# Routing tables, tile order and memory layout ahead of a mixture-of-experts loop

## The chip, the cores and the metric

The kernel runs on 1 core of one Trainium2 chip. The metric is the device time of one execution, from start to end, in microseconds (us); lower is better. Engines are PE (matmul), DVE (vector), ACT (scalar), POOL (GpSimd) and SP (which here only issues DMAs). POOL issues DMAs too.

## The reference

One decoder layer over 1024 prompt tokens and 8 sample tokens: S5 state space branch and sparse attention in parallel, an output projection with a post-norm, then a mixture of 32 experts, 4 of which each token uses. What the change touches is the expert routing:

```
logits = (x @ w_router).astype(F32) + b_router.astype(F32)
top_v, top_e = lax.top_k(logits, TOP_K)          # 4 experts of 32 for each token
...
counts = jnp.bincount(e, length=N_EXPERTS)
pcounts = (counts + blk - 1) // blk * blk
...
row_tok = jnp.full((rows,), n, jnp.int32).at[dest].set(tok_s)   # which token stands in which row
blk_e = jnp.minimum(jnp.searchsorted(pend, jnp.arange(n_blk) * blk, side='right'), N_EXPERTS - 1)
...
gate = jnp.minimum(gu[:, :D_FF], SWIGLU_LIMIT)   # per block: two products with the expert's weights
hh = (up + 1.0) * gate * jax.nn.sigmoid(SWIGLU_ALPHA * gate)
return hh @ w_down[ei] + b_down[ei]
```

## The kernel before

Tokens stand in 9 tiles: tiles 0 to 7 hold 128 prompt tokens each, tile NT = 8 holds the 8 sample tokens. The stages that matter run in this order.

**Output stage** (`post`). Three steps per tile: `glu(t)` (three tiles ahead), `outer(t)` (two halves of 24 products each, then DVE and ACT work for two norms, with the results `x1` and `hd` stored to DRAM) and `route(t)` (8 transposes of `h`, two ACT copies, the router products, then `choose`, nine small DVE steps to the top 4 experts, and a running count `cum`). The order on each engine is made by a planner. Tile 8 comes last. `mod` holds three rows of modulation; it is loaded for tile 0 and again, other values, for tile 8.

**Dispatch** (`dispatch`). From the counts: `rk`, the rank of each token within its expert (PE); the item table, one row of 4 numbers per work item, by some 30 small DVE steps; `slots`, called twice (a multiply-add to `sm`, a product `tmp` of 1152 numbers, its sum, a cast): once for the rows of the expert stage, once for `slot`, which only the last stage uses. Then 36 pairs of one-hot tiles `ol` and `ob` on DVE and 36 products into `ip` give `idx`, the token of each row. The item table goes to `tab` by way of DRAM (`tabd`), since it has to turn from 64 partitions into one.

**Expert loop** (`moe_raw`). Ahead of it, POOL issues, in this order: the load of `sel`, the loads of the first expert's gate and up weights into `raw[:,0:4]` (L110, eight of 1 MB), and zeros for `bc`, `st` and `ut`. Then a hand-synchronised section begins. SP goes into it first (L113): it waits for all that the section reads or writes, and then all engines start it. In it, POOL gathers tokens by `idx` (L421), ACT and DVE split weights into `hi` and `lo`, PE multiplies.

**Combine.** Gathers the rows back by `slot`, sums and norms; it already takes the sample's tile first.

**Memory.** Pools without a side are stacked from the left end of each partition, those with `side="right"` from the other. A left pool that closes gives its space to the next. So the pool of the output stage and the pool of the expert loop begin at the same byte. In bytes per partition, the output stage's pool begins with the two parts of `w_out` (65,536), `mod[0]`, `mod[1]`, `mod[2]` (4,096 each); the expert loop's begins with `sel` (2,048) and `raw` (98,304). The pool `di` of dispatch lies at the right end, and the last tiles of the expert loop's pool (`st`, `ut`, `sh`, `yt`, `bc`, `ic`) lie over it. A tile's first writer waits for the last readers of every tile that lay in any of its bytes (`reuse_waits="tile"`).

Of the kernel before, what the change touches and what calls it, by code (L numbers as in the profile page):

```python
# [22 lines left out]
D = 1024  # L23
# [59 lines left out]
def moe_raw(tc, x, wgu, wd, ydram, tab, idx, bsc, sel, ident, pools, NIT_MAX, NE=32):  # L83
# [10 lines left out]
    raw=sb.tile([128,6,4096],F,name="raw")  # L94
# [3 lines left out]
    st=sb.tile([128,2,2,256],F,name="st"); ut=sb.tile([128,2,2,256],F,name="ut")  # L98
    sh=sb.tile([128,2,512],F,name="sh")
    yt=sb.tile([128,2,1024],F,name="yt")  # L100
    bc=sb.tile([128,512],FR,name="bc")
    ic=sb.tile([128,2],I32,name="ic")
# [10 lines left out]
    with tc.tile_critical():  # L113
# [5 lines left out]
        def rawview(u):  # L119
            if u<16: return raw[:,u//4,u%4*1024:(u%4+1)*1024].rearrange("p (k f) -> p k f",k=2)  # L120
            C,k=DOWN[u-16]
            return raw[:,4+k//4].rearrange("p (k f) -> p k f",k=4)[:,k%4:k%4+2,C*512:(C+1)*512]
# [16 lines left out]
        with nc.Block() as block:  # L139
            @block.sync  # L140
            def _(eng):
                E=Eng(eng,nc,tab,W,NIT_MAX); i1=E.reg(1,1); i2=E.reg(2,1); pt=E.reg(W,W); ex=E.reg(); en=E.reg(); ep=E.reg(0); eq=E.reg(NE)
                def load(e,m):
                    if m<4:
                        src=wgu[bass.ds(e,1)].rearrange("o (k p) (h f) -> (o p) k h f",p=128,h=2)[:,:,:,m*256:(m+1)*256]
                        dst=raw[:,m].rearrange("p (k h f) -> p k h f",k=8,h=2)
                        for h in range(2): eng.dma_start(out=dst[:,:,h],in_=src[:,:,h]).then_inc(S['raw'][m],16)
                    else:
                        src=wd[bass.ds(e,1)].rearrange("o (k p) f -> (o p) k f",p=128)[:,(m-4)*4:(m-3)*4]
                        eng.dma_start(out=raw[:,m].rearrange("p (k f) -> p k f",k=4),in_=src).then_inc(S['raw'][m],32)  # L150
# [300 lines left out]
class K:  # L451
# [1360 lines left out]
    def post(self):  # L1812
# [4 lines left out]
        with ExitStack() as c:  # L1817
# [77 lines left out]
            def route(t):  # L1895
                n = rows(t)
                h = live.pop(t)
                ht = p.tile([128, 8, 128], F, name="ht")
                for k0 in (0, 4):
                    tp = q.tile([128, 4, 128], F, name="tph", bufs=1)  # L1900
                    for k in range(4):
                        pe.transpose(tp[:, k, :n], h[:n, (k0 + k) * 128:(k0 + k) * 128 + 128], self.ident[:n, :n])
                    A.activation(out=ht[:, k0:k0 + 4, :n], in_=tp[:, :, :n], func=AF.Copy)
                pr = q.tile([128, 32], F, name="pr", bufs=1)
                for k in range(8):
                    pe.matmul(pr[:n], lhsT=ht[:, k, :n], rhs=wr[:, k], start=k == 0, stop=k == 7)
                self.choose(t, n, pr, br)

            for t in range(AHEAD):
                glu(t)  # L1910
# [11 lines left out]
            for t in range(NT + 2):  # L1922
                if t == 1:
                    self.expert_bias(p)
                if t <= NT:
                    outer(t)
                if t + AHEAD <= NT:
                    glu(t + AHEAD)
                if t:
                    route(t - 1)  # L1930
# [6 lines left out]
    def dispatch_pools(self, ctx):  # L1937
# [15 lines left out]
        nc.sync.dma_start(out=self.tok, in_=self.i["k_token"])  # L1953
# [35 lines left out]
    def dispatch(self):  # L1989
# [4 lines left out]
        tabd = tc.dram_tile([65, 4], I32, name="tabd")  # L1994
        with ExitStack() as c:
            q = self.pool("diq", psum=True, ctx=c)

# [6 lines left out]
            for k, s in enumerate((7, 8, 6)):  # L2004
                v.tensor_scalar(out=ci[:, k], in0=rk[:, NTT], scalar1=float(2 ** s - 1), scalar2=None, op0=ALU.add)
                v.tensor_scalar(out=ci[:, k], in0=ci[:, k], scalar1=s, scalar2=None, op0=ALU.arith_shift_right)
            v.tensor_copy(out=cnt[:, 3], in_=rk[:, NTT])
            v.tensor_copy(out=cnt[:, 0:3], in_=ci)
            inc = p.tile([128, 4, 32], F, name="inc")
            exc = p.tile([128, 4, 32], F, name="exc")  # L2010
            for k in (0, 1, 3):
                v.tensor_tensor_scan(out=inc[:, k], data0=ones[:, 0:32], data1=cnt[:, k], initial=0.0, op0=ALU.mult, op1=ALU.add)
                v.tensor_tensor(out=exc[:, k], in0=inc[:, k], in1=cnt[:, k], op=ALU.subtract)

            n = 64
            m1 = p.tile([n, 32], F, name="m1")
            m2 = p.tile([n, 32], F, name="m2")
            v.tensor_scalar(out=m1, in0=exc[:n, 1], scalar1=row[:n], scalar2=None, op0=ALU.is_le)
            v.tensor_scalar(out=m2, in0=inc[:n, 1], scalar1=row[:n], scalar2=None, op0=ALU.is_gt)
            v.tensor_tensor(out=m1, in0=m1, in1=m2, op=ALU.mult)  # L2020
# [6 lines left out]
            v.tensor_tensor(out=j, in0=j, in1=pk[:, 4:5], op=ALU.mult)  # L2027
            it = p.tile([n, 4], F, name="it")

            v.tensor_scalar(out=it[:, 0:1], in0=pk[:, 4:5], scalar1=-31.0, scalar2=31.0, op0=ALU.mult, op1=ALU.add)  # L2030
            v.tensor_tensor(out=it[:, 0:1], in0=it[:, 0:1], in1=pk[:, 0:1], op=ALU.add)
            v.scalar_tensor_tensor(out=it[:, 1:2], in0=j, scalar=2.0, in1=pk[:, 2:3], op0=ALU.mult, op1=ALU.add)
            v.scalar_tensor_tensor(out=it[:, 2:3], in0=j, scalar=-4.0, in1=pk[:, 3:4], op0=ALU.mult, op1=ALU.add)
            v.tensor_scalar(out=it[:, 2:3], in0=it[:, 2:3], scalar1=2.0, scalar2=4.0, op0=ALU.max, op1=ALU.min)
            v.scalar_tensor_tensor(out=it[:, 3:4], in0=j, scalar=256.0, in1=pk[:, 5:6], op0=ALU.mult, op1=ALU.add)
            iti = p.tile([n, 4], I32, name="iti")
            v.tensor_copy(out=iti, in_=it)
            ni = p.tile([1, 4], I32, name="ni")
            v.tensor_copy(out=ni, in_=inc[0:1, 1, 31:32].to_broadcast([1, 4]))
# [7 lines left out]
            def slots(out, k, scale):  # L2047
                v.scalar_tensor_tensor(out=sm, in0=exc[:, k:k + 1].to_broadcast([128, NTT, 32]), scalar=scale, in1=rk[:, 0:NTT], op0=ALU.mult, op1=ALU.add)
# [5 lines left out]
            slots(vs, 0, 128.0)  # L2054
# [42 lines left out]
    def combine(self):  # L2097
# [3 lines left out]
        with ExitStack() as c:  # L2101
            p = self.pool("co", ctx=c)
            q = self.pool("coq", bufs=2, psum=True, ctx=c)
            row = lambda name, bufs: p.tile([128, D], F, name=name, bufs=bufs)

            def fetch(t):
                n = 128 if t < NT else B
                ys = []
                for k in range(4):
                    ys.append(row("y", 4 * LOOK + 8))  # L2110
                    g_.indirect_dma_start(out=ys[-1][:n], out_offset=None, in_=self.yd, in_offset=bass.IndirectOffsetOnAxis(ap=self.slot[:n, t, k:k + 1], axis=0))
# [35 lines left out]
            def weights(t, on):  # L2147
# [3 lines left out]
                pe.transpose(wt[:, :n], wr[:n, t], self.ident[:n, :n])  # L2151
# [20 lines left out]
            def rest(t, n, ys, x, pb, on):  # L2172

                acc, prev = row("acc", NTT), pb
                for k in range(on, 4):
                    v.scalar_tensor_tensor(out=acc[:n], in0=ys[k][:n], scalar=wk[:n, t, k:k + 1], in1=prev[:n], op0=ALU.mult, op1=ALU.add)  # L2176
# [143 lines left out]
```

## Time and profile before

| | |
|---|---|
| three runs | 3199.05, 3202.93, 3207.68 us (median 3202.93) |
| profiled execution | 3209.21 us, of which the span from first to last instruction is 3207.4 us |
| PE, DVE, ACT, POOL busy | 93%, 72%, 56%, 11% of the span |
| instructions | 51067 |

The profiled execution is 6.28 us above the median. The 1.8 us that are no part of its span lie around the first and the last instruction. All times in the text below are us from the start of the span.

### The profile page before, as it was taken

How to read it: one execution, taken by the hardware profiler on the slowest of the kernel's cores; microseconds unless marked ns; L12 is line 12 of the kernel's file. 1: busy time of each engine (PE TensorE's matmuls, PEld its weight loads, DVE VectorE, ACT ScalarE, POOL GpSimd, SP SyncE). 2: the span in 40 equal slices, each digit the busy share in tenths (PEclk: the TensorE clock that was granted, in tenths of full speed). 3: DMA queues.
4: the chain of work that ended last, by engine and by line, in shares of the span. 5: the costliest groups of instructions: out<-in, count | busy, mean ns of one | idle time of the engine just before them, and what ended most of it. 6: DMA issues, size and time to landing. Idle time of an engine off the chain costs nothing. (4 is left out here: it accounts for less than half of the span.)

```text
span 3207.4 us, 51067 instructions
## 1 busy us (share of the span) xinstructions
PE 2972.0 (93%) x15681; PEld 2380.6 (74%) x15682; DVE 2321.0 (72%) x4434; ACT 1785.9 (56%) x2824; POOL 358.7 (11%) x467
## 2 busy tenths in 40 slices
PE   7787899998999898599999999999999999999977
PEld 4555699976778586378887887888887888878752
DVE  5654846448777688688878868775689865796978
ACT  3332635456657643377667656564477654675751
POOL 1620121002311000100000000000000000000013
PEclk9888899988879799699999999999999999999988
DMA  8766343223512342798979869764289915792926
GB/s 287 250 219 226 126 124 106 85 74 83 132 29 65 126 152 80 264 335 288 315 228 369 277 230 360 233 238 139 77 281 371 337 68 190 242 368 100 350 84 275
DMA packets 445575, 656.33 MB, mean 205 GB/s; under 512 B 45455, under 2 KB 371072, under 8 KB 441265
## 3 DMA queue, kind: packets, MB, share of 16 engines
q1 hardware_dynamic: 418290, 535.40, 49.7%
q0 software_dynamic: 24464, 115.59, 10.4%
q10 hardware_dynamic: 2704, 3.85, 0.3%
q8 instruction: 64, 1.05, 0.1%
q14 instruction: 53, 0.43, 0.0%
HBM read 594.95 MB, written 68.73 MB: 207 GB/s over the span
## 5 line engine op out<-in xcount | busy, mean ns | idle before, releaser
L272 DVE TENSOR_TENSOR lo<-raw,hi 128x1024 fp32r<-128x1024 f32 x870 | 1030.9, 1221 | 307.3 <-ACT hi L199 302.3
L199 ACT ACTIVATE hi<-raw 128x1024 fp32r<-128x1024 f32 x870 | 916.3, 1060 | 491.9 <-PE pc L388 490.7
L386 PE MATMUL pc<-hi,X 128*128 128x512 f32 x1408 | 561.0, 398 | 4.7 <-DVE X L277 3.8
L388 PE MATMUL pc<-hi,X 128*128 128x512 f32 x1408 | 550.8, 391 | 0.0
L387 PE MATMUL pc<-lo,X 128*128 128x512 f32 x1408 | 549.8, 390 | 0.0
L386 PEld LDWEIGHTS pc<-hi,X 128*128 128x128 f32 x1408 | 265.2, 188 | 60.6 <-issue 8.9
L388 PEld LDWEIGHTS pc<-hi,X 128*128 128x128 f32 x1408 | 264.9, 188 | 56.6
L387 PEld LDWEIGHTS pc<-lo,X 128*128 128x128 f32 x1408 | 265.5, 189 | 51.5
L386 PE MATMUL pc<-hi,HT 128*128 128x512 f32 x704 | 282.6, 401 | 12.1 <-DVE HT L294 9.0
L388 PE MATMUL pc<-hi,HT 128*128 128x512 f32 x704 | 274.8, 390 | 0.0
L387 PE MATMUL pc<-lo,HT 128*128 128x512 f32 x704 | 274.6, 390 | 0.0
L386 PEld LDWEIGHTS pc<-hi,HT 128*128 128x128 f32 x704 | 132.2, 188 | 53.4 <-issue 28.5
L388 PEld LDWEIGHTS pc<-hi,HT 128*128 128x128 f32 x704 | 132.2, 188 | 28.3
L1319 DVE CUSTOM_DVE_ANT_0 pt<-sc,tt 128x512 f32<-128x512 f32 (+7 forms) x256 | 107.3, 436 | 61.5 <-PE sc L1335 29.1
L387 PEld LDWEIGHTS pc<-lo,HT 128*128 128x128 f32 x704 | 132.4, 188 | 24.9
L475 PE MATMUL po<-wih,hh 128*128 128x256 f32 (+3 forms) x504 | 147.6, 293 | 0.0
L476 PE MATMUL po<-wil,hh 128*128 128x256 f32 (+3 forms) x504 | 146.9, 292 | 0.0
L477 PE MATMUL po<-wih,hl 128*128 128x256 f32 (+3 forms) x504 | 145.8, 289 | 0.0
L504 PE MATMUL po<-wt,ct 128*9 128x256 f32 x384 | 102.6, 408 | 38.6 <-DMA wt<-in_w_ada_dram 36.9
L421 POOL DMA_INDIRECT xg<-hd,ic x52 | 65.4, 1257 | 589.2 <-PE px L354 558.2
L1157 ACT ACTIVATE xh<-tp 128x512 fp32r<-128x512 f32 x128 | 71.3, 594 | 89.1 <-PE tp L1155 80.6
L1372 PE MATMUL tp<-ident,pt 128*128 128x128 f32 (+6 forms) x592 | 115.3, 306 | 4.4 <-DVE pt L1358 4.0
(698 smaller groups left out, 5742.6 us busy)
## 6 DMA issues: line engine op xcount, KB each, us to landing
raw<-in_w_gate_up_dram SPq DMA_DIRECT2D x248, 1024.0 KB, 10.0
raw<-in_w_down_dram SPq DMA_DIRECT2D x64, 2048.0 KB
wt<-in_w_ada_dram SPq DMA_DIRECT2D x24, 1024.0 KB
yd<-yt SPq DMA_DIRECT2D x44, 512.0 KB
w<-ssmw SPq DMA_DIRECT2D x16, 512.0 KB
raw<-in_w_gate_up_dram POOLq DMA_DIRECT2D x8, 1024.0 KB
wir<-in_w_in_dram SPq DMA_DIRECT2D x20, 256.0 KB
bx<-bt SPq DMA_DIRECT2D x1, 4608.0 KB
```

The lines of the kernel that those rows point to most:

```text
L199: A.activation(out=hi[:,u%H],in_=rawview(u),func=AF.Copy).then_inc(S['hi'][u],1)
L272: V.tensor_tensor(out=lo[:,u%H],in0=rawview(u),in1=hi[:,u%H].bitcast(F),op=ALU.subtract).then_inc(S['lo'][u],1)
L386: PE.matmul(o,lhsT=sH,rhs=wh,start=kt==0,stop=False)
L387: PE.matmul(o,lhsT=sH,rhs=wl,start=False,stop=False)
L388: ins=PE.matmul(o,lhsT=sL,rhs=wh,start=False,stop=kt==7)
L475: pe.matmul(o, lhsT=lh, rhs=rh, start=start, stop=False)
L476: pe.matmul(o, lhsT=lh, rhs=rl, start=False, stop=False)
L477: return pe.matmul(o, lhsT=ll, rhs=rh, start=False, stop=stop)
L504: last = nc.tensor.matmul(po, lhsT=ct[:, k], rhs=wt[:, k], start=k == 0, stop=k == KT - 1)
L1157: nc.scalar.activation(out=xo, in_=tp, func=AF.Copy)
L1319: v.tensor_tensor_reduce(out=pt[:, off[r] + a:off[r] + a + n], in0=sc, in1=bias, scale=1.0, scalar=-3e38, op0=ALU.add, op1=ALU.max, accum_ ...
L1372: pe.transpose(tp[:n, h * 128:h * 128 + 128], pr[h][:, a:a + n], self.ident)
```

## The change

Tile order: `post` takes tile 8 first, and the tables by tile (`lg`, `oh`, `cum`, `slot`, ...) keep it at position 0. The item table is turned by four small products and a copy out of PSUM, not by DRAM. DVE's part of dispatch stands in written order. The one-hots are made for three tiles at a time by broadcasting, the token number is multiplied in by ACT, and the second `slots` stands behind `idx`. `sm`, the one-hots and two more tiles move from `di` to a new pool, `dis`, that has no side. In the expert loop's pool `raw` is cut to four slots, `st`, `ut`, `bc` and `ic` follow it, and the two slots for the down weights (`rawd`) stand at the end.

```diff
-    raw=sb.tile([128,6,4096],F,name="raw")
+    raw=sb.tile([128,4,4096],F,name="raw")
+    st=sb.tile([128,2,2,256],F,name="st"); ut=sb.tile([128,2,2,256],F,name="ut")
+    bc=sb.tile([128,512],FR,name="bc")
+    ic=sb.tile([128,2],I32,name="ic")
...
+    rawd=sb.tile([128,2,4096],F,name="rawd")
...
-                self.choose(t, n, pr, br)
+                self.choose((t + 1) % (NT + 1), n, pr, br)
...
+            seq = [NT] + list(range(NT))
+            for t in seq[:AHEAD]:
                 glu(t)
...
-                    outer(t)
+                    outer(seq[t])
...
+            p2 = self.pool("dis", ctx=c)
+            c.enter_context(tc.manual_schedule(engines={ET.DVE}))
...
-            for k, src in enumerate((io[:n, 0:32], exc[:n, 1], exc[:n, 0], cnt[:n, 2], ones[:n, 0:32], exc[:n, 3])):
-                v.tensor_tensor(out=m2, in0=m1, in1=src, op=ALU.mult)
-                v.tensor_reduce(out=pk[:, k:k + 1], in_=m2, axis=AX.X, op=ALU.add)
+            v.tensor_tensor(out=m6, in0=src[:n], in1=m1[:, 0:1].to_broadcast([n, 6, 32]), op=ALU.mult)
+            v.tensor_reduce(out=pk, in_=m6, axis=AX.X, op=ALU.add)
...
-            nc.sync.dma_start(out=tabd[1:65], in_=iti)
-            nc.sync.dma_start(out=tabd[0:1], in_=ni)
-            nc.sync.dma_start(out=self.tab, in_=tabd.rearrange("(o n) w -> o (n w)", o=1))
-            sm = p.tile([128, NTT, 32], F, name="sm")
+            tp = q.tile([1, 4, 64], F, name="tp")
+            for m in range(4):
+                pe.matmul(tp[:, m], lhsT=it[:, m:m + 1], rhs=self.ident[:n, :n], start=True, stop=True)
+            sm = p2.tile([128, NTT, 32], F, name="sm")
...
+            v.tensor_copy(out=self.tab[:, 4:260].rearrange("o (n m) -> o m n", m=4), in_=tp)
...
-            for t in range(NTT):
-                for k in range(4):
-                    ol = p.tile([128, 128], F16, name="ol", bufs=6)
-                    ob = p.tile([128, 72], F16, name="ob", bufs=6)
-                    v.tensor_scalar(out=ol, in0=self.io16, scalar1=hf[:, 1, t, k:k + 1], scalar2=None, op0=ALU.is_equal)
-                    v.tensor_scalar(out=ob, in0=self.io16[:, 0:72], scalar1=hf[:, 0, t, k:k + 1], scalar2=self.tok[:, t:t + 1], op0=ALU.is_equal, op1=ALU.mult)
-                    pe.matmul(ip, lhsT=ol, rhs=ob, start=t == 0 and k == 0, stop=t == NT and k == 3)
+            G = 3
+            for t0 in range(0, NTT, G):
+                both = []
+                for h, w in enumerate((72, 128)):
+                    o = p2.tile([128, G * 4, w], F16, name="ob" if h == 0 else "ol", bufs=3)
+                    bc = [128, G * 4, w]
+                    hs = hf[:, h, t0:t0 + G].rearrange("p t (k o) -> p (t k) o", o=1)
+                    v.tensor_tensor(out=o, in0=self.io16[:, None, 0:w].to_broadcast(bc), in1=hs.to_broadcast(bc), op=ALU.is_equal)
+                    if h == 0:
+                        for t in range(G):
+                            A.activation(out=o[:, 4 * t:4 * t + 4], in_=o[:, 4 * t:4 * t + 4], func=AF.Copy, scale=self.tok[:, t0 + t:t0 + t + 1])
+                    both.append(o)
+                for k in range(G * 4):
+                    pe.matmul(ip, lhsT=both[1][:, k], rhs=both[0][:, k], start=t0 + k == 0, stop=t0 + G == NTT and k == G * 4 - 1)
             v.tensor_copy(out=self.idx, in_=ip)
-            slots(self.slot, 3, 1.0)
+            slots(self.slot, 5, 1.0)
```

## Rows read from the trace of the kernel before

**Rows 1.** Windows: busy us of each engine, granted PE clock, DMA share, GB/s.

```profile
1133.00:1265.00 132.00, 131.99 (x682) 103.19 (x680) 114.62 (x297) 59.12 (x82) 0.00 (x0) 1.00 0.30 106
...
1292.90:1302.10 9.20, 0.01 (x1) 0.00 (x0) 9.15 (x38) 0.00 (x0) 0.05 (x1) 0.50 1.03 349
...
1342.50:1500.00 157.50, 156.42 (x720) 127.43 (x719) 134.96 (x171) 112.56 (x143) 9.88 (x13) 1.00 0.90 300
```

**Rows 2.** Timeline: POOL's issues and the end of dispatch (start, duration, engine, line).

```profile
1265.10 0.56 POOL L2093 DMA_DIRECT2D sel<-in_k_sel_dram  x1 [177.19 <-PE py L477]
...
1285.88 7.07 POOL L110 DMA_DIRECT2D raw<-in_w_gate_up_dram  x8 [20.22 <-DMA hd<-h]
...
1316.84 0.23 DVE L2070 CAST idx<-ip 128x72 int32<-128x72 f32 x1 [0.22 <-PE ip L2069]
1316.87 0.52 POOL L111 MEMSET bc<- 128x512 f32 x1 [23.92 <-PE ip L2069]
...
1318.22 0.95 POOL L112 MEMSET ut<- 128x1024 f32 x1
...
1323.69 1.05 POOL L421 DMA_INDIRECT xg<-hd,ic  x1 [1.18 <-issue]
```

**Rows 3.** The SP queue's waits, 1240 to 1340: total us, times, longest us.

```profile
SPq L113 <- DVE idx L2070: 2.9, 1, 2.9
SPq L113 <- POOL ut L112: 2.0, 1, 2.0
SPq L113 <- DMA tab<-tabd: 1.6, 1, 1.6
SPq L113 <- DMA raw<-in_w_gate_up_dram: 1.5, 2, 1.0
```

**Rows 4.** Instructions of L113, first and last start us.

```profile
L113 SPq EVENT_SEMAPHORE  x9: 28/28/2882, 1311.2 to 1317.1; - x9
L113 SPq NOP  x1: 18/18/18, 1319.2 to 1319.2; - x1
```

**Rows 5.** Timeline of DVE, output stage's end and dispatch.

```profile
1265.60 0.62 DVE L1886 TENSOR_TENSOR z<-py,md 8x512 f32<-8x512 f32 x1
...
1284.10 1.21 DVE L1810 TENSOR_TENSOR h<-h,md 8x1024 f32<-8x1024 f32 x1
...
1292.95 0.29 DVE L2005 TENSOR_SCALAR ci<-rk 128x32 int32<-128x32 f32 x2 [2.55 <-PE rk L2000]
...
1302.15 0.24 DVE L2067 TENSOR_SCALAR ol<-io,hf 128x128 f16<-128x128 f16 x1
```

**Rows 6.** Groups by line and shape: busy us, mean ns of one, idle before.

```profile
L2067 DVE TENSOR_SCALAR ol<-io,hf 128x128 f16<-128x128 f16 x36 | 9.0, 250 | 0.0
...
L2049 DVE TENSOR_TENSOR tmp<-oh,sm 128x1152 f32<-128x1152 f32 x2 | 2.7, 1352 | 0.0
...
L1903 ACT ACTIVATE ht<-tph 128x512 f32<-128x512 f32 x2 | 1.2, 597 | 3.8 <-PE tph L1902 3.7
...
L2048 DVE SCALAR_TENSOR_TENSOR sm<-exc,rk 128x288 f32<-128x288 f32 x2 | 0.9, 436 | 0.0
...
L2128 DVE TENSOR_TENSOR oh<-io,ef 128x1152 f32<-128x1152 f32 x1 | 1.3, 1282 | 0.0
```

**Rows 7.** Timeline: routing of tile 7, then of the sample's tile.

```profile
1275.05 1.09 PE L1902 MATMUL tph<-ident,h 128*128 128x128 f32 x4 [9.71 <-DVE h L1810]
...
1281.29 0.19 DVE L1978 TENSOR_TENSOR lg<-pr,br 128x32 f32<-128x32 f32 x1 [2.21 <-PE pr L1906]
...
1285.45 0.56 PE L1902 MATMUL tph<-ident,h 8*128 8x8 f32 x4 [4.20 <-DVE h L1810]
...
1287.94 0.18 DVE L1978 TENSOR_TENSOR lg<-pr,br 8x32 f32<-8x32 f32 x1 [2.64 <-PE pr L1906]
...
1288.89 0.55 DVE L1983 TENSOR_SCALAR ef<-ef,gone 128x4 f32<-128x4 f32 x1
```

**Rows 8.** Waits at the output stage's start, 1096 to 1135.

```profile
PE tpg L1850 <- DMA g<-yg: 9.0, 2, 7.9
```

More of the change, by code (lines that the diff above doesn't have):

```diff
@@ L121, in rawview @@
             C,k=DOWN[u-16]
-            return raw[:,4+k//4].rearrange("p (k f) -> p k f",k=4)[:,k%4:k%4+2,C*512:(C+1)*512]
+            return rawd[:,k//4].rearrange("p (k f) -> p k f",k=4)[:,k%4:k%4+2,C*512:(C+1)*512]
         def either(E,cls,f,*waits):
@@ L149, in load @@
                         src=wd[bass.ds(e,1)].rearrange("o (k p) f -> (o p) k f",p=128)[:,(m-4)*4:(m-3)*4]
-                        eng.dma_start(out=raw[:,m].rearrange("p (k f) -> p k f",k=4),in_=src).then_inc(S['raw'][m],32)
+                        eng.dma_start(out=rawd[:,m-4].rearrange("p (k f) -> p k f",k=4),in_=src).then_inc(S['raw'][m],32)
                 cl=E.reg(2); row=E.reg(0); y2=E.reg(1,1)
@@ L1971, in dispatch_pools @@
         self.mk = p.tile([128, NTT, 32], F, name="mk")
+        self.src = p.tile([128, 6, 32], F, name="src")
+        nc.gpsimd.tensor_copy(out=self.src[:, 0], in_=self.io[:, 0:32])
+        nc.gpsimd.memset(self.src[:, 4], 1.0)
         self.cum = p.tile([128, NTT + 1, 32], F, name="cum")
@@ L2005, in dispatch @@
                 v.tensor_scalar(out=ci[:, k], in0=rk[:, NTT], scalar1=float(2 ** s - 1), scalar2=None, op0=ALU.add)
+            v.tensor_copy(out=cnt[:, 3], in_=rk[:, NTT])
+            for k, s in enumerate((7, 8, 6)):
                 v.tensor_scalar(out=ci[:, k], in0=ci[:, k], scalar1=s, scalar2=None, op0=ALU.arith_shift_right)
-            v.tensor_copy(out=cnt[:, 3], in_=rk[:, NTT])
             v.tensor_copy(out=cnt[:, 0:3], in_=ci)
-            inc = p.tile([128, 4, 32], F, name="inc")
@@ L2010, in dispatch @@
[L2010 to L2013, printed above, removed]
-            n = 64
-            m1 = p.tile([n, 32], F, name="m1")
-            m2 = p.tile([n, 32], F, name="m2")
-            v.tensor_scalar(out=m1, in0=exc[:n, 1], scalar1=row[:n], scalar2=None, op0=ALU.is_le)
@@ L2019, in dispatch @@
-            v.tensor_scalar(out=m2, in0=inc[:n, 1], scalar1=row[:n], scalar2=None, op0=ALU.is_gt)
-            v.tensor_tensor(out=m1, in0=m1, in1=m2, op=ALU.mult)
+            src, inc, exc = self.src, p2.tile([128, 3, 32], F, name="inc"), (2, 1, 5)
+            for n, k in enumerate((0, 1, 3)):
+                v.tensor_tensor_scan(out=inc[:, n], data0=ones[:, 0:32], data1=cnt[:, k], initial=0.0, op0=ALU.mult, op1=ALU.add)
+            for n, k in enumerate((0, 1, 3)):
+                v.tensor_tensor(out=src[:, exc[n]], in0=inc[:, n], in1=cnt[:, k], op=ALU.subtract)
@@ new lines, in dispatch @@
+            v.tensor_copy(out=self.tab[:, 0:1], in_=inc[0:1, 1, 31:32])
+            n = 64
+            m1 = p.tile([n, 2, 32], F, name="m1")
+            m6 = p2.tile([n, 6, 32], F, name="m6")
+            v.tensor_scalar(out=m1[:, 0], in0=src[:n, 1], scalar1=row[:n], scalar2=None, op0=ALU.is_le)
+            v.tensor_scalar(out=m1[:, 1], in0=inc[:n, 1], scalar1=row[:n], scalar2=None, op0=ALU.is_gt)
+            v.tensor_copy(out=src[:n, 3], in_=cnt[:n, 2])
+            v.tensor_tensor(out=m1[:, 0], in0=m1[:, 0], in1=m1[:, 1], op=ALU.mult)
@@ L2026, in dispatch @@
             v.tensor_tensor(out=j, in0=row[:n], in1=pk[:, 1:2], op=ALU.subtract)
-            v.tensor_tensor(out=j, in0=j, in1=pk[:, 4:5], op=ALU.mult)
             it = p.tile([n, 4], F, name="it")
             v.tensor_scalar(out=it[:, 0:1], in0=pk[:, 4:5], scalar1=-31.0, scalar2=31.0, op0=ALU.mult, op1=ALU.add)
+            v.tensor_tensor(out=j, in0=j, in1=pk[:, 4:5], op=ALU.mult)
             v.tensor_tensor(out=it[:, 0:1], in0=it[:, 0:1], in1=pk[:, 0:1], op=ALU.add)
+            v.scalar_tensor_tensor(out=it[:, 2:3], in0=j, scalar=-4.0, in1=pk[:, 3:4], op0=ALU.mult, op1=ALU.add)
@@ L2047, in slots @@
             def slots(out, k, scale):
-                v.scalar_tensor_tensor(out=sm, in0=exc[:, k:k + 1].to_broadcast([128, NTT, 32]), scalar=scale, in1=rk[:, 0:NTT], op0=ALU.mult, op1=ALU.add)
+                v.scalar_tensor_tensor(out=sm, in0=src[:, k:k + 1].to_broadcast([128, NTT, 32]), scalar=scale, in1=rk[:, 0:NTT], op0=ALU.mult, op1=ALU.add)
                 v.tensor_tensor(out=tmp, in0=self.oh, in1=sm[:, :, None, :].to_broadcast([128, NTT, 4, 32]), op=ALU.mult)
@@ L2053, in dispatch @@
             vs = p.tile([128, NTT, 4], I32, name="vs")
-            slots(vs, 0, 128.0)
+            slots(vs, 2, 128.0)
+            v.tensor_copy(out=self.tab[:, 4:260].rearrange("o (n m) -> o m n", m=4), in_=tp)
             hl = p.tile([128, 2, NTT, 4], I32, name="hl")
@@ L2110, in fetch @@
                     ys.append(row("y", 4 * LOOK + 8))
-                    g_.indirect_dma_start(out=ys[-1][:n], out_offset=None, in_=self.yd, in_offset=bass.IndirectOffsetOnAxis(ap=self.slot[:n, t, k:k + 1], axis=0))
+                    g_.indirect_dma_start(out=ys[-1][:n], out_offset=None, in_=self.yd, in_offset=bass.IndirectOffsetOnAxis(ap=self.slot[:n, at(t), k:k + 1], axis=0))
                 x = row("x", LOOK + 2)
@@ L2150, in weights @@
                 wt = q.tile([32, 128], F, name="wt")
-                pe.transpose(wt[:, :n], wr[:n, t], self.ident[:n, :n])
+                pe.transpose(wt[:, :n], wr[:n, at(t)], self.ident[:n, :n])
                 wts = p.tile([32, 128], F, name="wts", bufs=NTT)
@@ L2175, in rest @@
                 for k in range(on, 4):
-                    v.scalar_tensor_tensor(out=acc[:n], in0=ys[k][:n], scalar=wk[:n, t, k:k + 1], in1=prev[:n], op0=ALU.mult, op1=ALU.add)
+                    v.scalar_tensor_tensor(out=acc[:n], in0=ys[k][:n], scalar=wk[:n, at(t), k:k + 1], in1=prev[:n], op0=ALU.mult, op1=ALU.add)
                     prev = acc
```

31 lines of the change are left out of this document (12 added, 19 removed).

## The prediction

> **What bounds the kernel now.** I read the windows by stage first. The output stage is bound by PE up to 1265, and the expert loop is bound by PE from 1342.5 on, at the full granted clock [rows 1]. Neither loses or gains work here. What the change can move is the stretch between them, 77 us in which PE does little: the tail of the output stage, dispatch, and the start of the loop. The granted clock is 0.50 there, in dispatch [rows 1], so at the lower of its two levels (1.2 of 2.4 GHz), after PE had run out of dense work.
>
> Next I read who ends that stretch. SP is the engine that opens the loop's section, so its queue's waits name the candidates [rows 3]. They add up: SP begins to wait at 1311.2 [rows 4], 1.6 for the item table, 1.5 for the weights of the first expert, 2.9 for `idx`, 2.0 for the last zeroed tile, and 1311.2 + 8.0 = 1319.2 is when the section opens [rows 4]. So the weights had landed at about 1311.2 + 1.6 + 1.5 = 1314.3, the table at 1312.8, `idx` at 1317.07 [rows 2], and the zeros of `ut` came last, since `bc` waits for the last product into `ip` [rows 2]. The four lie within 7 us, so whoever speeds up one must ask about the others.
>
> Of these the weights are the heavy one. POOL issues them from 1285.88 [rows 2] and they land 1314.3 - 1285.9 = 28.4 us later, of which 8.39 MB at the 349 GB/s of the window [rows 1] are 24.0. They are hidden today because they start before dispatch and run under it.
>
> **What released the weights.** `sel` went out at 1265.10, when the products that read `w_out` were over; the eight loads behind it only at 1285.88 [rows 2]. That is right behind the end of L1810 at 1284.10 + 1.21 = 1285.3 [rows 5], which reads `mod[1]`. `mod[1]` lies at byte 69,632 of that pool, while `raw[:,0:4]`, the part loaded, ends at 67,584. So the wait is for the whole tile `raw`, not for the part written. This is the rule by which I read the new layout.
>
> **The weights after the change.** `raw` has four slots now: with `sel` it covers 67,584 bytes, that is both parts of `w_out` (65,536) and half of `mod[0]`, last read by L1886 at 1265.60 [rows 5]. So far the load could start some 20 us earlier. But dispatch has a new pool, `dis`, without a side. It opens after the output stage's pool has closed and before the loop's opens, so it begins at the same byte as both. It holds 384 + 768 + 1152 + 3 x 1728 + 3 x 3072 = 16,704 bytes: `inc`, `m6`, `sm`, and the one-hots. `sel` and the front of `raw` lie over it. `sm` is last read in the second `slots`, which now stands behind `idx`; the one-hots by the last products into `ip`. So `sel`, and behind it on POOL's queue all eight loads and the three zeroings, wait until dispatch is over. The load that ran under dispatch now follows it.
>
> The Trainium skill speaks of this (DMA: Bandwidth & Descriptors, Anatomy of one DMA — SWDGE path): DMA engines do not wait on semaphores; the wait stands in the issuing sequencer, before dispatch of the DMA. By that rule one held load holds every issue behind it; the 20.22 us in which POOL stood idle ahead of L110 [rows 2] agree.
>
> **Dispatch itself, term by term.**
> Before: DVE starts at 1292.95, the first one-hot at 1302.15 [rows 5], `idx` ends at 1317.07 [rows 2], 24.1 us in all.
> After, up to the item table: some 27 small steps, a price that the windows bound from below: of the 38 steps in the 9.2 us before the one-hots [rows 1], six are the large ones of both `slots` (2 x 0.44 + 4 x 1.35 = 6.3), so the other 32 took 0.09 apiece, mixed so that few waited for the one ahead. In a written order many do; from above I take 0.2, the whole duration of a small step. The middle, 0.15, gives 4.1.
> The first `slots`: 0.44 [rows 6] + 1.35 [rows 6] + the sum over the same 1152 numbers at the same price + a small cast, 3.4 with the gaps.
> The copy of the turned table: 256 numbers on one partition, priced as the 288 numbers of `sm`, 0.4 [rows 6]. The four products that feed it are hidden under `slots`. Three integer steps and a cast 0.6. Together 8.5, where before it was 9.2.
> The one-hots: three groups of 12 x 72 and 12 x 128 numbers. The nearest row is the same comparison with the same broadcasts in f32, 1152 numbers in 1.28 us [rows 6], or 1.11 ns a number: 864 take 0.96, 1536 take 1.71, three groups 8.0; with the usual overlap of 0.1 a step, 7.6. ACT's three scalings a group are 288 numbers each, against 0.60 for 512 [rows 6], about 1.1 to 1.3 a group, under DVE's `ol` of 1.71.
> The last 12 products and the cast: the LDWEIGHTS and products of before followed DVE at its pace, so their own is not shown; between 0.1 and 0.25 us apiece, I take 0.15 and 0.45 for the cast: 2.2.
> Sum 4.1 + 4.4 + 7.6 + 2.2 = 18.3, a gain of 5.8. If f16 halved the one-hots it would be 9.6; if every step of the written order stalled and the products ran at 0.25, 3.1.
>
> The Trainium skill (VectorE: DVE Perf Modes, The perf-mode tier table) gives a two-tensor step on 16-bit data in SBUF twice the rate of f32, if both read neighbours with step 1. Here one input repeats a single number along the row, which leaves the plain rate. No row shows such a step in f16. By the double rate the time below would be 3.8 us less.
>
> The DRAM trip of the item table is removed at no gain: it landed at 1312.8, 4.3 us ahead of `idx`. But without it `idx` can move.
>
> **The output stage in another order.** PE's work is the same. At the end the last tile is now a full one. Its way from the first transpose to `lg` took 1281.29 - 1275.05 = 6.24, the sample's 1287.94 - 1285.45 = 2.49 [rows 7], so 3.75 more, less the 0.6 step L1983 that only the sample has [rows 7]: +3.2. At the start, PE waited 7.9 us for the first `g` [rows 8], which for the sample is 1/16 of the bytes, but the weights of the gate have to come too. I take 1.0 of gain (0 to 3). The rows of `mod` for the prompt are now loaded in the second tile; a tile takes some 14 us of PE and `mod[0]` is free after its first use, so I cost that at nothing; without that cover it would be a load of 2 to 3 us. Sum +2.2 (0 to 4).
>
> **The opening of the section.** `idx` would end at 1317.07 - 5.8 + 2.2 = 1313.5. The second `slots` reads `sm` until 0.44 + 1.35 later, 1315.3. `sel` takes 0.56 and a gap, then the loads go out at 1316.1 and land 28.4 later: 1344.5. That is 25.3 behind 1319.2. The zeros follow the loads on POOL (8 x 0.9, then 2.4) and are long done. The second `slots` itself ends on DVE some 27 us before it could matter. The gather and the start of the loop then run as before.
>
> Profiled execution 3209.2 + 25.3 = 3234.5; it lies 6.3 above the median of the runs shown, so I forecast 3202.9 + 25.3 = 3228. About 0.3%, 9.6 us, is what a measurement here can tell from no change; this is beyond it.
>
> **Rivals.**
> A, not slower: the loads are not held by `dis` (because it lies elsewhere, or the wait is not drawn). Then they go out at about 1266, land before 1295, and `idx` opens the section: -5.8 + 2.2 - 2.0 (zeros no longer last) = -5.6, 3197; with the one-hots at half price and no loss in the tail -11.6, 3191. It decides itself by where the first load stands: if it goes out more than 28 us ahead of `idx`, this is the case. For it: the layout was cut so that `raw` is free early. Against it: L110's wait in the trace follows the bytes, and the loop's pool leaves no room beside `dis`.
> B, a part only: the loads wait by the slots that they write, and only `sel` and the first slot (2.1 MB) are late. Then 1315.3 + 0.8, 6.0 for the bytes and the 4.4 that the eight loads took beyond theirs: 1326.5, +7.3, 3210. Against it: L110 waited for `mod[1]`, which the part written does not touch.
>
> **Chances and range.** Forecast 0.84, A 0.10 (of it 0.02 beyond 0.3% faster), B 0.06 (0.01 beyond 0.3% slower). Slower 0.85, same 0.13, faster 0.02. Within the forecast: dispatch 3.1 to 9.6, tail 0 to 4, and the load some 3 us shorter if nothing else moves data: +18 to +30, with the 4 us by which runs differ on each side 3217 to 3237. That leaves out A and B, 0.16.
>
> **What would show it.** Right: L2093 and L110 behind the second `slots`' product, not at 1265; a window of some 28 us with DMA share near 1.0 and every engine idle; SP's wait at L113 for `raw` about 28 us long, no wait for `ut` or `tab`. Wrong: L110 ahead of `rk`; or a wait for `idx` that still ends last. The one-hots are right at 0.9 and 1.6 us a step. The tail is right if the last `lg` stands 6 us behind its first transpose.

## The result and the profile after

The changed kernel took 3241.05 us (median of 6 runs, 3227.28 to 3246.25), the kernel before 3205.69 in the same comparison (6 runs, 3199.05 to 3212.96). The ratio is 1.0101, interval [1.0075, 1.0126]: slower, by the mechanism that was forecast, and 4 us beyond the range. The profiled execution took 3241.38, its span is 3239.1.

POOL's timeline of the changed kernel, over the whole stretch from 1255 to 1360:

```profile
1319.73 0.56 POOL L2111 DMA_DIRECT2D sel<-in_k_sel_dram  x1 [226.63 <-DVE tmp L2058]
1320.62 7.07 POOL L111 DMA_DIRECT2D raw<-in_w_gate_up_dram  x8 [0.33 <-issue]
...
1329.01 1.00 POOL L113 MEMSET ut<- 128x1024 f32 x1
...
1352.69 1.05 POOL L422 DMA_INDIRECT xg<-hd,ic  x1 [1.18 <-issue]
```

The row of `sel` names what held it: `tmp` of L2058, the product in the second `slots`, the last reader of `sm`. Before, `sel` was out at 1265.10 and the loads at 1285.88 [rows 2]; now both leave 2.6 us and more behind the cast to `idx` (1317.08). POOL had stood idle for 226.63 us with the eight loads queued behind one transfer of 0.56. The trace agrees with the rule of the Trainium skill (DMA: Bandwidth & Descriptors, Anatomy of one DMA — SWDGE path), that the wait stands in the issuing sequencer. That such a wait holds every issue behind it is what these two rows show.

The waits of SP's queue from 1240 to 1360, and the instructions of L114 (L113 before), which open the section:

```profile
SPq L114 <- DMA raw<-in_w_gate_up_dram: 58.3, 3, 52.7
```

```profile
L114 SPq NOP  x2: 18/18/18, 1348.2 to 3139.0; - x2
```

Of the four candidates [rows 3] one is left. The wait is longer than the 28 us that were forecast, because without the trip of the item table SP reaches this line early, at 1348.2 - 58.3 = 1289.9; what counts is from the issue to the opening, 1348.2 - 1320.62 = 27.6.

Windows over dispatch, the load, the start of the loop and the loop, with busy us of PE, weight loads, DVE, ACT and POOL, the granted PE clock, the DMA share and GB/s:

```profile
1297.30:1317.30 20.00, 6.08 (x48) 3.96 (x48) 16.07 (x46) 4.15 (x9) 0.00 (x0) 0.50 0.00 0
1320.60:1348.20 27.60, 0.00 (x0) 0.00 (x0) 0.07 (x1) 0.00 (x0) 9.39 (x11) 0.50 0.95 313
1348.20:1366.40 18.20, 1.94 (x8) 1.57 (x8) 8.13 (x7) 8.41 (x9) 2.98 (x5) 0.50 0.69 264
1372.00:1529.50 157.50, 156.59 (x719) 126.89 (x718) 135.80 (x173) 112.92 (x144) 9.47 (x13) 1.00 0.90 300
```

The first two lines are the loss in one picture. Under dispatch the DMA engines moved nothing, where before they moved 349 GB/s [rows 1]; then they moved the weights for 27.6 us while PE and ACT did nothing. The last line is the loop at the same rates as before [rows 1].

DVE's timeline through dispatch:

```profile
1299.82 0.39 DVE L2014 TENSOR_SCALAR ci<-rk 128x32 int32<-128x32 f32 x3 [2.55 <-PE rk L2009]
...
1303.67 0.43 DVE L2057 SCALAR_TENSOR_TENSOR sm<-src,rk 128x288 f32<-128x288 f32 x1
...
1308.09 1.05 DVE L2080 TENSOR_TENSOR ob<-io,hf 128x864 f16<-128x864 f16 x1
1309.06 1.75 DVE L2080 TENSOR_TENSOR ol<-io,hf 128x1536 f16<-128x1536 f16 x1
...
1317.08 0.23 DVE L2087 CAST idx<-ip 128x72 int32<-128x72 f32 x1 [1.00 <-PE ip L2086]
...
1317.71 1.36 DVE L2058 TENSOR_TENSOR tmp<-oh,sm 128x1152 f32<-128x1152 f32 x1
```

From DVE's start to the end of `idx` it is 17.5 us, where 18.3 were forecast and 24.1 were taken before [rows 2, 5].

And the tail of the output stage, PE's first transposes of the last tile and DVE's `lg`:

```profile
1289.15 1.09 PE L1903 MATMUL tph<-ident,h 128*128 128x128 f32 x4 [4.22 <-DVE h L1811]
```

```profile
1295.39 0.19 DVE L1985 TENSOR_TENSOR lg<-pr,br 128x32 f32<-128x32 f32 x1 [6.39 <-PE pr L1907]
```

These are 6.24 us apart, as for tile 7 before [rows 7].

### The profile page after: what moved, and what is told of

It reads as the page before. It is cut to its first block, busy times and chain, and to the rows that moved or that the text cites. A ratio compares the mean times of both kernels' runs of the same rounds, so it can differ in the third digit from the quotient of the medians.

```text
span 3239.1 us, 51018 instructions
## 1 busy us (share of the span) xinstructions
PE 2968.0 (92%) x15689; PEld 2374.3 (73%) x15690; DVE 2317.2 (72%) x4359; ACT 1791.7 (55%) x2833; POOL 359.5 (11%) x469
## 3 DMA queue, kind: packets, MB, share of 16 engines
q8 instruction: 64, 1.05, 0.1%
## 5 line engine op out<-in xcount | busy, mean ns | idle before, releaser
L273 DVE TENSOR_TENSOR lo<-raw,hi 128x1024 fp32r<-128x1024 f32 x582 | 695.0, 1222 | 262.5 <-ACT hi L200 257.4
L200 ACT ACTIVATE hi<-raw 128x1024 fp32r<-128x1024 f32 x582 | 617.8, 1063 | 332.1 <-PE pc L389 330.7
L387 PE MATMUL pc<-hi,X 128*128 128x512 f32 x1408 | 562.4, 399 | 4.7 <-DVE X L278 3.8
L273 DVE TENSOR_TENSOR lo<-rawd,hi 128x1024 fp32r<-128x1024 f32 x288 | 340.2, 1220 | 72.5 <-ACT hi L200 72.5
L200 ACT ACTIVATE hi<-rawd 128x1024 fp32r<-128x1024 f32 x288 | 300.6, 1060 | 160.4 <-PE pc L389 160.4
L387 PEld LDWEIGHTS pc<-hi,X 128*128 128x128 f32 x1408 | 264.8, 188 | 62.5 <-issue 8.8
L387 PE MATMUL pc<-hi,HT 128*128 128x512 f32 x704 | 283.0, 402 | 9.9 <-DVE HT L295 8.9
L387 PEld LDWEIGHTS pc<-hi,HT 128*128 128x128 f32 x704 | 132.2, 188 | 49.7 <-issue 24.9
L388 PEld LDWEIGHTS pc<-lo,HT 128*128 128x128 f32 x704 | 132.4, 188 | 25.3
```

The lines of the kernel that those rows point to most:

```text
L200: A.activation(out=hi[:,u%H],in_=rawview(u),func=AF.Copy).then_inc(S['hi'][u],1)
L273: V.tensor_tensor(out=lo[:,u%H],in0=rawview(u),in1=hi[:,u%H].bitcast(F),op=ALU.subtract).then_inc(S['lo'][u],1)
L387: PE.matmul(o,lhsT=sH,rhs=wh,start=kt==0,stop=False)
L388: PE.matmul(o,lhsT=sH,rhs=wl,start=False,stop=False)
```

## The experiments

Each kernel was timed against the kernel before on the same chip. The times of one kernel scatter by up to 29 us, so a few us are read from the stages of the profile, not from the ratio. The stages are cut at these starts: the last store of `attd` (the end of the stage ahead; up to there PE, DVE and ACT run the same instructions in the same order in the kernels, and POOL and SP differ only by a few small steps and loads in the last 10 us), the last `z` (L1886, L1887 after), the last `cum`, the cast to `idx`, the opening of the section, the first and the last start of L386 (L387 with the new layout), the products into `pc` of the loop; the last column but one is what follows. So "to cum" is the tail of the output stage, "to idx" is dispatch, and "to opening" is what the section still waits for once `idx` is there. "To the end" is from the last `attd` to the end of the span.

| kernel | last attd at | to z | to cum | to idx | to opening | to 1st pc | loop | rest | to the end |
|---|---|---|---|---|---|---|---|---|---|
| before | 1096.1 | 169.5 | 24.6 | 26.6 | 2.4 | 17.6 | 1763.2 | 107.4 | 2111.3 |
| after | 1099.5 | 167.9 | 29.7 | 20.0 | 31.1 | 18.2 | 1764.8 | 107.9 | 2139.6 |
| e1 | 1093.7 | 167.9 | 30.0 | 19.9 | 3.6 | 17.9 | 1764.9 | 107.6 | 2111.8 |
| e2 | 1087.3 | 169.8 | 24.3 | 26.6 | 29.1 | 15.4 | 1762.8 | 108.1 | 2136.1 |
| e3 | 1102.3 | 169.1 | 24.3 | 20.0 | 31.0 | 18.2 | 1765.6 | 108.7 | 2136.9 |
| e4 | 1095.3 | 169.3 | 29.7 | 20.0 | 31.2 | 18.1 | 1765.9 | 108.9 | 2143.1 |
| e5 | 1102.5 | 169.8 | 24.3 | 20.0 | 3.5 | 17.7 | 1765.5 | 108.1 | 2108.9 |
| e6 | 1101.3 | 168.5 | 30.0 | 26.6 | 2.4 | 17.7 | 1762.5 | 107.4 | 2115.1 |
| e7 | 1092.4 | 170.2 | 24.3 | 26.6 | 0.4 | 17.4 | 1765.3 | 107.8 | 2112.0 |
| e8 | 1103.5 | 169.2 | 24.6 | 20.0 | 4.4 | 19.0 | 1763.0 | 107.9 | 2108.1 |
| e9 | 1101.2 | 168.3 | 24.3 | 20.0 | 3.6 | 17.6 | 1766.3 | 107.5 | 2107.6 |
| e10 | 1093.2 | 169.0 | 24.3 | 20.0 | 3.6 | 18.8 | 1765.4 | 107.4 | 2108.5 |
| e11 | 1099.7 | 168.9 | 24.2 | 20.0 | 3.6 | 18.4 | 1765.9 | 107.0 | 2108.0 |
| e12 | 1084.6 | 169.5 | 24.3 | 20.0 | 4.4 | 18.1 | 1762.1 | 107.9 | 2106.3 |

The first column says how far runs differ before what was changed has run: 19 us. From there to the end the same kernel (after and e4) repeats within 3.5 us, and the four columns from "to cum" to "to 1st pc" within 0.1.

**e1, the pool `dis` at the right end (after, one edit).**

```diff
-            p2 = self.pool("dis", ctx=c)
+            p2 = self.pool("dis", ctx=c, side="right")
```

> The changed kernel with the pool dis at the right end, where no byte of sel or raw lies over it. Theory (the held load is the loss): the eight loads go out within a few us of the last use of mod[0], near 1268, land before 1300, and the section opens at the end of the second slots, 3.4 us behind idx. From the changed kernel's stages: opening 1317.3 + 3.4 = 1320.7 in place of 1348.2, so 27.5 us less than the changed kernel, and against the kernel before +3.5 (tile order) - 6.6 (dispatch) + 1.3 (opening behind slots instead of zeros) = -1.8 us, ratio 0.999. Rival (the loss is in the steps of dispatch, the new order or the new places of the loop's tiles): at least 14 us of the loss stay, ratio 1.004 or more.

3211.21 us against 3211.02, ratio 1.0008 [0.9991, 1.0024]: the loss is gone with one word. POOL's timeline of e1, and SP's waits:

```profile
1261.91 0.56 POOL L2111 DMA_DIRECT2D sel<-in_k_sel_dram  x1 [174.53 <-PE py L478]
1262.78 7.07 POOL L111 DMA_DIRECT2D raw<-in_w_gate_up_dram  x8 [0.31 <-issue]
```

```profile
SPq L114 <- DVE sf L2059: 20.3, 1, 20.3
SPq L114 <- DMA raw<-in_w_gate_up_dram: 10.4, 3, 4.1
```

The loads leave behind the last products of the output stage, 52 us ahead of the opening, which now waits for the second `slots`: `rawd`, the last tile of the loop's pool, lies over `tmp` in `di`, and the sum `sf` is the last reader of `tmp`. Still e1 gains nothing over before: dispatch is 6.7 us shorter, and the longer tail, a later opening and a longer loop take it back.

**e2, the one-hots alone in such a pool (before, one edit).**

```diff
+            p2 = self.pool("dis", ctx=c)
...
-                    ol = p.tile([128, 128], F16, name="ol", bufs=6)
-                    ob = p.tile([128, 72], F16, name="ob", bufs=6)
+                    ol = p2.tile([128, 128], F16, name="ol", bufs=6)
+                    ob = p2.tile([128, 72], F16, name="ob", bufs=6)
```

> The kernel before with one edit: the one-hot tiles of dispatch lie in a left pool, under sel and the first bytes of raw. Everything else, each DVE step and the tile order too, as before. Theory: sel goes out behind the last product into ip, 1316.8, the loads from 1317.6, landing 27.5 to 28.4 later, the section opens at 1345 to 1346: +26 us, ratio 1.008. Rival (the loop can begin with part of the weights, so that most of the wait is hidden): under +10 us, ratio under 1.003.

3235.05 us, ratio 1.0069 [1.0045, 1.0094]. POOL's timeline and SP's waits of e2:

```profile
1308.55 0.56 POOL L2094 DMA_DIRECT2D sel<-in_k_sel_dram  x1 [229.47 <-issue]
1309.53 7.07 POOL L110 DMA_DIRECT2D raw<-in_w_gate_up_dram  x8 [0.42 <-issue]
```

```profile
SPq L113 <- DMA raw<-in_w_gate_up_dram: 38.8, 2, 36.2
```

Nothing was computed otherwise, not a byte more was moved, and the same 8.39 MB left 1.5 us behind the cast to `idx` (1308.0), where before they left 31 us ahead of it [rows 2]. The opening stands 29.1 us behind `idx`, in place of 2.4.

**e3, the sample's tile last again (after), and e4, after once more.** e3 turns back every line that has to do with the order; these two carry it:

```diff
-                self.choose((t + 1) % (NT + 1), n, pr, br)
+                self.choose(t, n, pr, br)
...
-            seq = [NT] + list(range(NT))
+            seq = list(range(NT + 1))
```

> The changed kernel with the sample's tile last again in the output stage (and its place in the tables as before). Theory: the tail of the output stage is 3.5 us shorter, all else stays, the load is still held: about 3.5 us less than the changed kernel, ratio to the kernel before 0.001 under that of the changed kernel in the same call. Rival (the order is free, the stages differ by the run): no difference.

> The changed kernel once more, beside the others. Theory (stage sums: load +28.8, dispatch -6.6, order +3.5): +26 us, ratio 1.008; the 3.4 us by which the part ahead of the output stage was late is of that one run and goes. Rival (a further loss of 7 to 10 us outside these stages belongs to the change): ratio 1.0105 or more, and the part ahead of the output stage or the loop is late again.

e3 took 3235.66 us, ratio 1.0069 [1.0049, 1.0089], e4 3241.64, ratio 1.0091 [1.0069, 1.0113]. The tail is 24.3 us with the sample last, as before, and 29.7 with it first. The ratio of e4 lies between the two readings and its interval holds both, so the times of e4 don't decide. Its stages give each reading a part: the part ahead is not late (1095.3, before 1096.1), but from the opening on e4 takes 4.7 us more than before (0.5, 2.7 and 1.5), which the theory had left out.

**e5, e1 with the sample last: what stays is the new dispatch and the loop's new layout.**

```diff
-            p2 = self.pool("dis", ctx=c)
+            p2 = self.pool("dis", ctx=c, side="right")
...
-            seq = [NT] + list(range(NT))
+            seq = list(range(NT + 1))
...
```

> After with two edits: the pool dis at the right end, and the sample's tile last again. What stays of the change is the new dispatch and the new layout of the loop's tiles. Theory (every loss located so far is a separate term): dispatch -6.6, the section opens some 3.6 us behind idx in place of 2.4 (+1.2), the start of the loop +0.5, the loop itself some 2 us longer under the new layout; together about -3, a ratio of 0.999, and the stretch from the last routing count to the first product of the loop 5 us shorter than before. Rival (the new dispatch gains its 6.6 in full, and nothing in the new layout costs anything): -6.6, a ratio of 0.998, with a loop of 1763 us from first to last product. The interval of the ratio is some 0.0015 either way, so the stages in the trace decide, not the ratio.

3209.08 us against 3213.08, ratio 0.9993 [0.9976, 1.0010]. Dispatch gave its 6.6, the opening took 1.1, the loop 2.3: to the end 2.4 us less than before.

**e6, the sample's tile first and nothing else (before).**

```diff
-            for t in range(AHEAD):
+            seq = [NT] + list(range(NT))
+            for t in seq[:AHEAD]:
...
```

> Before with one edit: the sample's tile first in the output stage. Theory (the order costs more than the 2.2 us of the prediction): the last z to the last count takes 29 to 30 us in place of 24.6, up to 1.6 are given back at the stage's start, so +3.5 to +5, a ratio of about 1.0013; the loads of the first expert go out as before, when the last tile has read mod[1], and stay hidden. Rival (the order is neutral and the longer tail of after came from its new dispatch): a tail of 24.6 to 25, a ratio of 1.000.

3211.64 us, ratio 1.0003 [0.9984, 1.0022]. The tail grew to 30.0 with the old dispatch behind it, so the order alone makes it, and 1.0 came back at the stage's start: 3.8 us to the end.

**e7, the loop's new layout alone (before), and e8, the new dispatch alone.**

```diff
-    raw=sb.tile([128,6,4096],F,name="raw")
+    raw=sb.tile([128,4,4096],F,name="raw")
+    st=sb.tile([128,2,2,256],F,name="st"); ut=sb.tile([128,2,2,256],F,name="ut")
+    bc=sb.tile([128,512],FR,name="bc")
+    ic=sb.tile([128,2],I32,name="ic")
...
+    rawd=sb.tile([128,2,4096],F,name="rawd")
...
```

e8 is e5 without these lines.

> Before with the loop's tiles laid out as after does it (raw in four slots, the zeroed tiles behind it, the slots for the down weights at the end), nothing else. Theory (the 2 us by which the loop is longer after come from this layout): the loads go out near 1266, the section opens with idx, 2 us earlier than before, and the loop takes 1765 us from first to last product in place of 1763; together 0, a ratio of 1.000. Rival (the loop's 2 us come with the order of the rows that dispatch makes, or are scatter): a loop of 1763, and -2 in all, a ratio of 0.9994, which the times alone cannot tell from none.

> Before with the new dispatch alone (item table turned by products, one-hots in three groups, second slots behind idx, the pool dis at the right end); the order of the tiles and the loop's layout are those of before. Theory (the layout is what lengthens the loop): a loop of 1763 us, idx 20 us behind the last count in place of 26.6, and the zeroed tiles, which lie over dispatch's space here, end last again, some 5 us behind idx; together about -4 us, a ratio of 0.9988, the fastest of the four. Rival (the loop's 2 us come with the new dispatch): a loop of 1765, and -2, a ratio of 0.9994.

e7 took 3209.46 us, ratio 0.9994 [0.9973, 1.0014]; e8 3206.26, ratio 0.9984 [0.9966, 1.0001]. With the layout the loads leave at 1263.5 and the section opens 0.4 behind `idx`, but the loop takes 1765.3; without it the loop takes 1763.0 with the new dispatch too. So it is the layout that lengthens the loop. Groups of the loop's products by shape, e8 and then e7 (busy us, mean ns of one, then PE's idle time before them):

```profile
L386 PE MATMUL pc<-hi,X 128*128 128x512 f32 x1408 | 560.9, 398 | 4.7 <-DVE X L277 3.8 <-issue 0.9
L388 PE MATMUL pc<-hi,X 128*128 128x512 f32 x1408 | 550.9, 391 | 0.0
```

```profile
L387 PE MATMUL pc<-hi,X 128*128 128x512 f32 x1408 | 562.6, 400 | 4.7 <-DVE X L278 3.9 <-issue 0.9
L389 PE MATMUL pc<-hi,X 128*128 128x512 f32 x1408 | 552.2, 392 | 0.0
```

The extra time is no wait: each product with `X` is about 1 ns longer, some 0.3%, at the same granted clock of 1.00.

**e9 to e12: what in the layout makes the loop longer.** e9 is e5 with 32 bytes more ahead of `hi`, e10 is e5 with `rawd` right behind `raw`, e11 has both; e12 is e8 with the cut of `raw` but every tile at its old byte.

```diff
-    ic=sb.tile([128,2],I32,name="ic")
+    ic=sb.tile([128,10],I32,name="ic")[:,0:2]
```

```diff
     raw=sb.tile([128,4,4096],F,name="raw")
+    rawd=sb.tile([128,2,4096],F,name="rawd")
...
-    rawd=sb.tile([128,2,4096],F,name="rawd")
```

> The kernel of e5 with one edit: 32 bytes more in ic, so that hi, lo, xg, X, HT and all behind them begin 32 bytes further on, at 32 modulo 64 as in before (in after they begin at 0 modulo 64). Theory (where these tiles begin within 64 bytes is what makes the products with X 1.2 ns longer in after): the loop takes 1763 us from first to last product, and the stretch from the output stage's last start to the end is 4.5 us shorter than before. Rival (it is the place of the slots for the down weights, or of X, in the partition): the loop stays at 1765.5, as in e5.

> The kernel of e5 with one edit: the slots for the down weights right behind the four of raw, where before had them; hi, X and HT begin 32,768 bytes further on, still at 0 modulo 64. By the theory of e9 (the begin within 64 bytes) the loop stays at 1765.5 us. By its rival (the place in the partition) it falls to 1763. The section opens 3.5 us behind idx in both, since sh and yt now lie over dis at the right end.

> The kernel of e5 with both edits of e9 and e10. Either theory of the loop gives 1763 us here; a loop of 1765 would refute both. With the loop back, the new dispatch gains all that is left of it: -6.6 in dispatch, +1.1 at the opening, together about -5 us against before, a ratio of 0.9985.

> The kernel of e8 with one edit: raw cut into four slots and rawd behind it, so that every tile of the loop keeps the byte at which before has it. Theory for the loop, after e9 to e11 have refuted the first two (it is the place of the zeroed tiles st, ut and bc): 1763 us from first to last product. Rival (it is the cut of the tile itself, whatever the bytes): 1765.5. For the opening: the loads go out near 1270 again, 20 us earlier than in e8, and the zeros of ut, which lie over dispatch's space, end last, some 5 us behind idx; the stretch to the end is 3 to 4 us shorter than before.

| kernel | time, us | before, us | ratio and interval | loop, us |
|---|---|---|---|---|
| e9 | 3208.23 | 3209.80 | 0.9997 [0.9983, 1.0012] | 1766.3 |
| e10 | 3207.50 | 3209.80 | 0.9999 [0.9984, 1.0015] | 1765.4 |
| e11 | 3211.87 | 3209.80 | 1.0006 [0.9989, 1.0024] | 1765.9 |
| e12 | 3205.60 | 3212.47 | 0.9982 [0.9967, 0.9996] | 1762.1 |

To the end, e9 to e11 take 2.8 to 3.7 us less than before, which their ratios can't tell from nothing. The loop stays at 1765.4 to 1766.3 in all three: neither the begin within 64 bytes nor the place of the down slots, nor both together, brings 1763 back. e12 rules out the cut of the tile. Over all fourteen profiles the loop takes 1762.1 to 1763.2 us wherever `st`, `ut`, `bc` and `ic` stand behind `HT`, and 1764.8 to 1766.3 wherever they stand ahead of `hi`; e5 to e8, on one chip, show both. But what stands ahead of `hi` also moves it. In the five short loops `hi`, `X` and `HT` have the bytes that they have before (`hi` begins 2,048 + 98,304 = 100,352 bytes into the pool); in the nine long ones they stand some 22,500 bytes earlier, or 10,300 later (e10, e11). So e10 and e11 did not test the place of `X`, the other half of the rival named for e9. No run moves the four tiles and leaves the operands where they were: whether the place of the four or that of the operands is the cause stays open, and so does how either lengthens a product.

e12 is the fastest version: of the nine kernels without the held load it is the only one whose interval leaves out 1, by 0.0004, which among nine trials is weak. Its POOL timeline, and under it the load of e8:

```profile
1253.57 0.56 POOL L2110 DMA_DIRECT2D sel<-in_k_sel_dram  x1 [175.07 <-PE py L478]
1255.00 7.07 POOL L111 DMA_DIRECT2D raw<-in_w_gate_up_dram  x8 [0.87 <-DVE m L1985]
...
1301.81 0.95 POOL L113 MEMSET ut<- 128x1024 f32 x1 [1.28 <-DVE sf L2058]
```

```profile
1293.01 7.07 POOL L110 DMA_DIRECT2D raw<-in_w_gate_up_dram  x8 [20.21 <-DMA hd<-h]
```

The loads leave 1.4 us behind `sel`, 43 us ahead of `idx` (1298.4), where in e8, with every tile at the same byte, they leave 20.8 behind `sel` (1272.23). So the wait goes by the whole tile, as the prediction read it. But the zeros of `ut` end last in both, and the section opens 4.4 us behind `idx` in both: the cut gives the load slack, and no time. To the end e12 takes 5.0 us less than before and e8 3.2; the 1.8 between them lie in the loop and its start, which the cut does not touch, and are less than the 3.5 by which one kernel repeats. What both gain is the new dispatch.

## Why the prediction was right in kind and short in size

**The held load: right.** `dis` begins at the byte of `sel` and reaches into `raw`, the last reader of `sm` released `sel`, and the section opened with the load: 31.1 us behind `idx` in place of 2.4. That is +28.7 at this place, where the forecast had 25.3 - 2.2 + 5.8 = 28.9. Of its two parts, the issue came 3.3 us behind the end of `idx` (1320.6 - 1317.3; forecast 1316.1 - 1313.5 = 2.6) and the opening 27.6 behind the issue (28.4 forecast); that these two errors cancel is luck. e1 takes the hold away and the loss goes; e2 adds the hold alone and the loss comes. Rival A fell: L111 did not leave ahead of dispatch. Rival B could not have come out: `sel` stands first in POOL's queue, so by the prediction's own rule what holds `sel` holds all eight loads. It is e12 against e8 that shows the wait for the whole tile.

**Dispatch: right.** 6.6 us shorter, 5.8 forecast. The steps up to `sm` took 1303.67 - 1299.82 = 3.9 (4.1), from there to the first one-hot 4.4 (4.4), the one-hots 8.0 (7.6), the last products and the cast 1.2 (2.2). The one-hots ran at 1.05 and 1.75 us, 1.1 to 1.2 ns a number: the plain rate. The page of the Trainium skill that the prediction weighed (VectorE: DVE Perf Modes, The perf-mode tier table) gives such a step on 16-bit data twice the rate; with an input that repeats one number the trace does not show it, as the prediction had read it.

**The output stage's order: the term was mis-sized.** "Sum +2.2 (0 to 4)" came out at 29.7 - 24.6 = +5.1 in the tail and -1.6 to -0.2 at the start (after and e4), together +3.5 to +4.9; e6, which has this part alone, gives +5.4 - 1.0 = +4.4. (What the start gives back is not clear of scatter: with the sample last "to z" lies between 168.3 and 170.2.) The step that was costed, the last route at full size, was right: 6.24 us. Missing was what lies ahead of it. The first transposes of the last tile stand 1289.15 - 1267.39 = 21.8 us behind its last `z`, against 1285.45 - 1265.60 = 19.9 before [rows 5, 7]. DVE's timeline of after shows where 1.8 of it is:

```profile
1267.39 0.69 DVE L1887 TENSOR_TENSOR z<-py,md 128x512 f32<-128x512 f32 x1 [0.31 <-PE py L478]
1268.00 1.28 DVE L518 BATCH_NORM_STATS2 bnst<-z 128x6 f32<-128x512 f32 x2
...
1269.86 1.17 DVE L1888 SCALAR_TENSOR_TENSOR z<-x,z 128x1024 f32<-128x1024 f32 x1
```

The next step on the last `z`, L1888, starts 2.5 us behind L1887, since the statistics of the tile ahead stand between them in the planner's order; with the sample last that gap is 0.7 (1266.31 - 1265.60 in before). Here the stage that ended with its smallest tile also ended with the shorter queue on DVE.

**The loop and its start: a term that was not there.** "The gather and the start of the loop then run as before", and the first part said of the output stage and the loop: "Neither loses or gains work here." The loop has the same work, but takes 1.6 to 2.7 us longer (after and e4). e7, e8 and e12 put that on the places of the tiles in the new layout. Its start takes 0.5 to 0.6 longer, which is no more than it scatters (17.4 to 19.0 in the kernels without the held load).

**The base: the step that failed most.** Of the profiled execution the prediction says: "it lies 6.3 above the median of the runs shown, so I forecast 3202.9 + 25.3 = 3228." The sum made against the profiled execution itself was 3234.5, and the same +18 to +30 with the same 4 us on each side would have been 3223 to 3243, with 3241.05 inside. The median of three runs was low: over 6 to 35 runs the kernel before took 3205.7 to 3213.1, around the profiled 3209.2, not 6.3 below it. (The medians of 17 to 35 runs are of other chips; draw and chip are not told apart.) The 12.8 us between 3228.2 and 3241.05 are 2.8 by which before moved in the same comparison (3205.69 - 3202.93) and 10.1 by which the difference of the medians, 35.4, was larger than the sum. From the last `attd` to the end the change cost 28.3 us in after and 31.8 in e4, 3.0 and 6.5 above the sum: the order and the loop account for 2.9 and 5.4 of that (3.5 - 2.2 + 1.6 and 4.9 - 2.2 + 2.7), and in e4 another 1.5 lies behind the loop (108.9 in place of 107.4). What remains of the 10.1 fits the scatter of the part ahead, where the last `attd` falls anywhere from 1084.6 to 1103.5 with nothing of weight changed ahead of it; e4 repeats the comparison with 30.6 between the medians. So the sum itself was 3.0 to 6.5 short, by the order and the loop in the main; the rest of the miss is where medians of three and six runs fell. The "4 us by which runs differ on each side" was too little: 35 runs of before lie from 3197.0 to 3222.8.

The sum by stages closes: -1.6 + 5.1 - 6.6 + 28.7 + 0.6 + 1.6 + 0.5 = 28.3, and 3.4 more from the last `attd`, make the 31.7 between the two spans.

## What to carry to other kernels

Before a scratch pool is put where a closed pool lay, ask which prefetch writes those bytes next, and which queue issues it: one late reader there held 8.39 MB and everything behind it on POOL, 28 us for 16.7 KB a partition, and the other end of the partition cost nothing. A cut of a tile lets what is written early leave without waiting for bytes that are freed late, and it can be had without moving a byte, as e12 shows; it pays only where that load is what the next stage waits for, and in e12 it was not. Make the sum against the execution from which its durations come, and read a change of a few us from stages between two fixed instructions; here a median of three runs lay 3 us below that of six, and up to 10 below those of more runs on other chips.

## What the runs showed that was not expected

With `st`, `ut`, `bc` and `ic` ahead of `hi`, and `hi`, `X` and `HT` therefore at other bytes, the products with `X` are longer at the same clock: 399 to 400 ns in place of 398 for L386 with `hi` and `X` (L387 in the new layout), over 1408 of them 562.0 to 562.8 us in place of 560.6 to 561.0, and 2.8 us of the loop in the mean (1765.5 over nine profiles, 1762.7 over five). Which of these places does it is not shown.

The part of the program ahead of the change, where PE, DVE and ACT run the same instructions in the same order, took 1084.6 to 1103.5 us up to the last `attd` in fourteen profiles, 1.7% of its length, while the loop of 1763 us repeats within 1.1 us for one layout.
